# Modulation weights in four buffers of their own, loaded one visit ahead, and both scaled sums on VectorE in four pieces

## The chip, the cores and the metric

The kernel runs on one core of a Trainium2 chip. The metric is the device time of one execution in microseconds (us); the lower the better. The engines are written as in the profile: PE is TensorE (PEld its weight loads), DVE VectorE, ACT ScalarE, POOL GpSimd, SP SyncE, which here issues the transfers.

## The reference, cut to what matters

Two layers (`l` is 0 or 1) of a transformer-like block over 256 latent and 256 context tokens, width 1024. Each layer is a feed-forward block, a token mixer and a second feed-forward block. Before and after each of them the tokens are modulated with vectors that come from two conditioning vectors, `c` for the latent tokens and `c_ctx` for the context tokens:

```python
mx = (silu(c) @ w_mod[l] + b_mod[l]).reshape(B, 9, 1, 1024)
mc = (silu(c_ctx) @ w_mod[l] + b_mod[l]).reshape(9, 1024)
hx = hx + 0.5 * mx[:, 2] * swiglu(modulate(hx, norm_g[l, 0], mx[:, 0], mx[:, 1]), w_gu[l, 0], w_down[l, 0])
...
hx = hx + mx[:, 5] * (ox @ w_out[l])
hx = hx + 0.5 * mx[:, 8] * swiglu(modulate(hx, norm_g[l, 2], mx[:, 6], mx[:, 7]), w_gu[l, 1], w_down[l, 1])
```

`w_mod[l]` has 1024 rows and 9 x 1024 columns, 4 MB for each of the nine vectors `m`; it is used for two input vectors only. `swiglu` is `(silu(x @ gate) * (x @ up)) @ down` with an inner width of 2816.

## The kernel before

**Weights.** All weights come from memory in a fixed list of units (`plan`, line 141). A unit of kind `gu` is 128 gate and 128 up columns (1 MB, two transfers), `down` is 256 output columns of a third of the inner width (1 MB or 768 KB), `mod` is 256 columns of one modulation vector for PE (1 MB), and `dvm` is half of such a quarter for the other engines: two row blocks of 128 by 512 columns (512 KB). Which vectors go by `dvm` is the list `ELEM` (line 35): six of layer 0, and of layer 1 the vectors 0, 4, 3, 5 and 7.

**Loading.** `take` (line 269) hands out the next unit. It first calls `load_to(i + 3)`, which puts the transfers of this unit and of the next two into SP's queue, whatever their kind: `raw` has three buffers, `draw` (for `dvm`) three of 512 KB. SP works its queue in order, and a transfer waits there until its buffer is free.

**Splits.** Matmuls run three times on values that are split in a rounded part and a rest (`mm3`, line 309: lines 312 to 314). `split` (line 254) makes both parts of a weight unit, in two halves: ACT copies (line 265), DVE subtracts (line 266). `spl` has two buffers. `take` splits its own unit if that isn't done, and then calls `ahead` (line 284), which splits the next unit that needs it, but looks no further than two units on.

**The feed-forward loop** (`ffn`, line 733). For each of 22 `gu` units: 48 matmuls of 128x512 (or 128x256 in the last block), `silu` on ACT (line 756), the product `hv` on DVE (line 758), a copy on ACT (line 760) and the rest on POOL (line 761). After 8, 16 and 22 of them four `down` units of 48 or 36 matmuls follow, with four additions of 128x256 on DVE (line 822). After every third step of three matmuls `step` (line 326) is called: it runs one entry of the list `dv`, and then one entry of `q` or one tick of the background work `bg`. In the first block of each layer `bg` is `s5_prep` (line 834), the preparation of the state-space mixer, mostly tensor operations on POOL. Between two units `fillers` (line 301) runs the modulation units that stand there in the list: one `mod` or two `dvm`. So 44 places have two `dvm` in a row; such a place is called a visit. 24 of them lie in the first block of layer 0 (after 16 `gu` and 8 `down` units), 4 in the second, 16 in the first block of layer 1. In 8 of the last 16 only one of the two sums is made.

**What a `dvm` unit does** (`dvm_unit`, line 515). For each of its two row blocks, a sum for `c` on DVE (lines 530 and 532: `acc = raw * scalar + acc`), and one for `c_ctx` in two steps, a scaling on ACT in place (line 535) and an addition on POOL (line 537). All of it is written out at once. After four units PE sums over the partitions (`total`, line 547) and later transposes (`finish`), seven and ten steps on.

**Order.** Nothing is reordered: each engine runs its instructions in the order in which the Python code writes them out.

Of the kernel before, what the change touches and what calls it, by code (L numbers as in the profile page):

```python
# [94 lines left out]
class Net:  # L95
    def __init__(self, nc, tc, I, out, es):
        self.nc, self.tc, self.I, self.out, self.es = nc, tc, I, out, es
        pool = lambda n, b=1, **kw: es.enter_context(tc.tile_pool(name=n, bufs=b, **kw))
        sb = lambda n, b=1: es.enter_context(lines(tc, name=n, bufs=b))
        self.const = sb("const")  # L100
        self.rawp = sb("raw", 3)
        self.splp = sb("spl", 2)
        es.enter_context(tc.tile_pool(name="top", bufs=1, side="right")).tile([128, 8], F32, name="top")
        self.pacc = pool("pacc", 4, space=PSUM)
        self.pt = pool("pt", 3, space=PSUM)
        self.pm = pool("pm", 1, space=PSUM)
        self.bank, self.turn = None, 0
        self.dram = pool("dram", 1, space=DRAM)
        c = self.const
        self.k = c.tile([128, K_END], F32, name="k")  # L110
        self.ident = self.k[:, K_ID:K_ID + 128]
        self.ones = self.k[:, K_ONE:K_ONE + 128]
        self.h = c.tile([128, KT, T], F32, name="h")
        self.xn = c.tile([128, 2, KT, T], F32R, name="xn")
        self.cs = c.tile([128, KT, 38], F32, name="cs")
        self.mh = c.tile([128, 8], F32, name="mh")
        self.sel = c.tile([128, 33], F32, name="sel")
        self.mod = [c.tile([128, 9, KT, 2], F32, name=f"mod{l}") for l in range(2)]
        self.A = [c.tile([128, 3, KT, 2], F32, name=f"A{l}") for l in range(2)]
        self.smT = [c.tile([128, 128], F32, name=f"smT{l}") for l in range(2)]  # L120
        self.kg = [c.tile([128, 4], F32, name=f"kg{l}") for l in range(2)]
        self.rho8 = [c.tile([128, 16], F32, name=f"rho8{l}") for l in range(2)]
        self.units = []
        self.dv = []
        self.fp = None
        self.bg = []
        self.q = []
        self.hold = False
        self.seaming = False
# [11 lines left out]
    def plan(self):  # L141
        I = self.I
        U = self.units

        def mod_units(l, m, us=range(4)):
            for u in us:
                if (l, m) in ELEM:
                    for v in (2 * u, 2 * u + 1):
                        n0, k0 = m * 1024 + v // 4 * 512, v % 4 * 2
                        src = I["w_mod"][l].rearrange("(k p) n -> p k n", p=128)[:, k0:k0 + 2, n0:n0 + 512]  # L150
                        U.append(("dvm", (l, m, v), [(slice(0, 1024), 2, src)], False))
                    continue
                src = I["w_mod"][l].rearrange("(k p) n -> p k n", p=128)[:, :, m * 1024 + u * 256:m * 1024 + u * 256 + 256]
                U.append(("mod", (l, m, u), [(slice(0, 2048), 8, src)], False))

# [12 lines left out]

        def ffn(l, f, fill, skip=0, between=None):
            fill = list(fill)  # L170
            for c in range(3):
                for j in range(max(skip, sum(CH[:c])), sum(CH[:c + 1])):
                    gu(l, f, j)
# [49 lines left out]
    def load_to(self, n):  # L223
        while self.loaded < min(n, len(self.units)):
            i = self.loaded
            kind, key, srcs, sp = self.units[i]
            if kind == "dvm" and self.fp is None:
                return
            if i < 10 and kind == "mod":
                raw = self.prop.tile([128, 2048], F32, name="pmod", tag="pmod", bufs=5)  # L230
            elif kind == "dvm":
                raw = self.fp.tile([128, 1024], F32, name="draw", tag="draw", bufs=3)
            else:
                raw = self.rawp.tile([128, 2048], F32, name="raw", tag="raw")
            for sl, k, src in srcs:
# [33 lines left out]
    def take(self, kind, key, ahead=True):  # L269
# [3 lines left out]
        if self.hold:  # L273
            self.load_to(min(i + 8, 11))
        else:
            self.load_to(i + 3)
        self.split(i)
        if ahead and not self.hold:
            self.ahead()
# [46 lines left out]
    def step(self, n=1):  # L326

        for _ in range(n):
            if self.dv:
                g = self.dv.pop(0)  # L330
                if g:
                    g()
            f = self.q.pop(0) if self.q else None
            if f is not None:
                f()
            else:
                self.tick()
# [6 lines left out]

    def dv_flush(self):
        while self.dv:
            g = self.dv.pop(0)
            if g:
                g()

    def drain(self):
        while self.bg:
# [159 lines left out]
            us = [u] if alone else range(4)  # L512
            self.q.append(lambda: self.mod_finish(l, m, us, e))

    def dvm_unit(self, l, m, v):

        nc = self.nc
        half, r = v // 4, v % 4  # L520
        raw = self.take("dvm", (l, m, v)).rearrange("p (k n) -> p k n", k=2)
        ss = (1,) if l and m > 4 else (0, 1)
        if r == 0:
            self.dacc = {s: self.fp.tile([128, 512], F32, name=f"dacc{s}", tag=f"dacc{s}", bufs=2) for s in ss}
        acc = self.dacc
        for i in range(2):
            c0, c1 = (self.cs[:, 2 * r + i, 6 + s:7 + s] for s in range(2))
            first = r == i == 0
            if first:
                nc.vector.tensor_scalar(acc[1], raw[:, i], c1, None, op0=OP.mult)  # L530
            else:
                nc.vector.scalar_tensor_tensor(acc[1], raw[:, i], c1, acc[1], op0=OP.mult, op1=OP.add)  # L532
            if 0 in ss:
                x = acc[0] if first else raw[:, i]
                nc.scalar.activation(x, raw[:, i], AF.Copy, scale=c0)  # L535
                if not first:
                    nc.gpsimd.tensor_tensor(acc[0], acc[0], x, op=OP.add)  # L537
        if r < 3:
            return
        st = {}  # L540

# [17 lines left out]
            nc.vector.tensor_tensor(dst.rearrange("p (j a) s -> p a j s", a=2), t, bc(b, [128, 2, 2, 2]), op=OP.add)  # L559
            self.mod_derived(l, m, k0, k0 + 4)  # L560

        self.dv_flush()
        self.dv += [None] * 7 + [total, None, None, finish]

    def mod_derived(self, l, m, k0, k1):
        nc = self.nc
# [166 lines left out]
    def ffn(self, l, f, halves, started, nxt=None):  # L733
# [3 lines left out]
        gate = 2 if f == 0 else 8  # L737
        hid = {}
        with lines(self.tc, name=f"ffn{l}{f}", bufs=1) as fp:
            self.fp = fp  # L740
            j0 = 0
            for ci, nf in enumerate(CH):
                for j in range(j0, j0 + nf):
# [10 lines left out]
                                    self.step()  # L754
                    sl = fp.tile([128, T], F32, name="sl", tag="sl", bufs=1)
                    nc.scalar.activation(sl[:, c], pg[:, c], AF.Silu)
                    hv = fp.tile([128, T], F32, name="hv", tag="hv", bufs=2)
                    nc.vector.tensor_tensor(hv[:, c], sl[:, c], pu[:, c], op=OP.mult)  # L758
                    hd = fp.tile([128, 2, T], F32R, name="hid", tag="hid", bufs=8)
                    nc.scalar.activation(hd[:, 0, c], hv[:, c], AF.Copy)  # L760
# [7 lines left out]
                    self.sq_begin()  # L768
                early = None
                if lastc:  # L770
                    self.dv_flush()
                for u in range(4):
                    w = early or self.take("down", (l, f, ci, u))
                    w = w[:, :, 0:nf * 256].rearrange("p s (k n) -> p s k n", k=nf)
# [22 lines left out]
                            self.step()  # L797
                    if ci == 0 and u == 0:
                        self.flush()
                    for i in range(2):  # L800
                        n = 2 * u + i
                        for s in halves:
# [31 lines left out]
    def s5_prep(self, l):  # L834
# [6 lines left out]
        with lines(self.tc, name=f"prep{l}", bufs=1, side="right") as pp:  # L841
# [4 lines left out]
            dma(par[0:16], I["s5_lam_re"][l].rearrange("d (a b) p -> (d a) (b p)", b=2))  # L846
            dma(par[32:48], I["s5_lam_im"][l].rearrange("d (a b) p -> (d a) (b p)", b=2))
            dma(ldt[64:80], I["s5_log_dt"][l].rearrange("d (a b) -> (d a) b", b=2))
            bl = [pp.tile([128, 16, 16], F32, name=f"bl{i}") for i in range(2)]
            for i, nm in enumerate(("s5_b_re", "s5_b_im")):  # L850
                nc.sync.dma_start(bl[i], I[nm][l].rearrange("d (a b) p m -> (b p) (d a) m", b=2))
            cr = pp.tile([128, 4, 2, 2, 64], F32, name="cr", tag="W")
# [824 lines left out]
```

## Time and profile before

| | |
|---|---|
| median of 3 runs | 2185.57 us (2183.81 to 2187.68) |
| profiled execution | 2195.32 us, of which the span of the trace is 2193.5 us |
| mean granted clock of PE | 0.938 |
| PE busy | 1984.7 us, 90% of the span |
| DVE busy | 1109.0 us, 51% |
| ACT busy | 784.7 us, 36% |
| POOL busy | 767.9 us, 35% |
| read from memory | 263.39 MB, 126 GB/s over the span |

The shares are averages over a program with very different stages. What a stage is limited by is read from the idle time of PE inside it, from what ended that idle time, and from the clock that PE was granted there. The modulation visits lie in three stretches of the trace: about 60 to 490 us, 905 to 980 us and 1305 to 1600 us.

### The profile page before, as it was taken

How to read it: one execution, taken by the hardware profiler on the slowest of the kernel's cores; microseconds unless marked ns; L12 is line 12 of the kernel's file. 1: busy time of each engine (PE TensorE's matmuls, PEld its weight loads, DVE VectorE, ACT ScalarE, POOL GpSimd, SP SyncE). 2: the span in 40 equal slices, each digit the busy share in tenths (PEclk: the TensorE clock that was granted, in tenths of full speed). 3: DMA queues.
4: the chain of work that ended last, by engine and by line, in shares of the span. 5: the costliest groups of instructions: out<-in, count | busy, mean ns of one | idle time of the engine just before them, and what ended most of it. 6: DMA issues, size and time to landing. Idle time of an engine off the chain costs nothing. (4 is left out here: it accounts for less than half of the span.)

```text
span 2193.5 us, 27710 instructions
## 1 busy us (share of the span) xinstructions
PE 1984.7 (90%) x10839; PEld 1600.1 (73%) x10839; DVE 1109.0 (51%) x1777; ACT 784.7 (36%) x1283; POOL 767.9 (35%) x789
## 2 busy tenths in 40 slices
PE   7788778889999999989999997778899999899999
PEld 5656556667889568768888875555678888668999
DVE  6566433543655774343332455555543465575554
ACT  4432333332435553331222343321222343455443
POOL 2348766431444404140100224864520244503000
PEclk9888888899999999989999998888899999899999
DMA  7533444454443103443333354344463344308663
GB/s 257 139 116 130 140 135 146 131 162 134 121 157 101 39 4 112 124 143 98 96 96 87 106 140 116 115 134 144 148 188 87 101 132 144 88 20 235 188 190 118
DMA packets 342278, 277.73 MB, mean 127 GB/s; under 512 B 30558, under 2 KB 311460, under 8 KB 342148
## 3 DMA queue, kind: packets, MB, share of 16 engines
q1 hardware_dynamic: 339184, 268.44, 41.2%
q0 software_dynamic: 1888, 7.31, 0.9%
q8 instruction: 85, 1.39, 0.3%
q14 instruction: 45, 0.37, 0.1%
q10 hardware_dynamic: 1076, 0.22, 0.1%
HBM read 263.39 MB, written 12.55 MB: 126 GB/s over the span
## 5 line engine op out<-in xcount | busy, mean ns | idle before, releaser
L312 PE MATMUL acc<-xn,spl 128*128 128x512 f32 (+1 forms) x1664 | 625.3, 376 | 96.3 <-ACT spl L265 87.9
L314 PE MATMUL acc<-xn,spl 128*128 128x512 f32 (+1 forms) x1664 | 617.2, 371 | 20.7 <-DVE spl L266 20.7
L313 PE MATMUL acc<-xn,spl 128*128 128x512 f32 (+1 forms) x1664 | 611.6, 368 | 1.9 <-DVE xn L429 0.2
L266 DVE TENSOR_TENSOR spl<-raw,spl 128x1024 fp32r<-128x1024 f32 (+2 forms) x312 | 391.9, 1292 | 231.5 <-ACT spl L265 229.6
L312 PEld LDWEIGHTS acc<-xn,spl 128*128 128x128 f32 x1664 | 329.0, 198 | 164.9 <-ACT spl L265 98.7
L265 ACT ACTIVATE spl<-raw 128x1024 fp32r<-128x1024 f32 (+3 forms) x344 | 323.8, 989 | 260.3 <-PE acc L314 138.5
L314 PEld LDWEIGHTS acc<-xn,spl 128*128 128x128 f32 x1664 | 327.4, 197 | 89.0 <-DVE spl L266 40.0
L761 POOL TENSOR_TENSOR hid<-hv,hid 128x512 fp32r<-128x512 f32 (+1 forms) x88 | 102.1, 1160 | 783.9 <-ACT hid L760 783.8
L313 PEld LDWEIGHTS acc<-xn,spl 128*128 128x128 f32 x1664 | 329.1, 198 | 54.6 <-DVE xn L658 4.3
L312 PE MATMUL acc<-hid,spl 128*128 128x512 f32 (+1 forms) x740 | 273.3, 369 | 28.8 <-ACT spl L265 28.8
L314 PE MATMUL acc<-hid,spl 128*128 128x512 f32 (+1 forms) x740 | 270.0, 365 | 10.5 <-DVE spl L266 10.5
L313 PE MATMUL acc<-hid,spl 128*128 128x512 f32 (+1 forms) x740 | 268.8, 363 | 0.0
L758 DVE TENSOR_TENSOR hv<-sl,acc 128x512 f32<-128x512 f32 (+1 forms) x88 | 54.6, 621 | 391.5 <-PE acc L314 344.6
L537 POOL TENSOR_TENSOR dacc<-dacc,draw 128x512 f32<-128x512 f32 x126 | 187.2, 1485 | 158.7 <-ACT draw L535 106.8
L822 DVE SCALAR_TENSOR_TENSOR h<-acc,mod,h 128x256 f32<-128x256 f32 x192 | 84.8, 478 | 226.4 <-PE acc L314 226.4
L760 ACT ACTIVATE hid<-hv 128x512 fp32r<-128x512 f32 (+1 forms) x88 | 50.8, 577 | 391.1 <-DVE hv L758 391.1
L312 PEld LDWEIGHTS acc<-hid,spl 128*128 128x128 f32 x740 | 144.0, 195 | 55.4 <-ACT spl L265 32.5
L314 PEld LDWEIGHTS acc<-hid,spl 128*128 128x128 f32 x740 | 144.3, 195 | 37.4 <-DVE spl L266 16.5
L532 DVE SCALAR_TENSOR_TENSOR dacc<-draw,cs,dacc 128x512 f32<-128x512 f32 x154 | 164.0, 1065 | 4.7
L313 PEld LDWEIGHTS acc<-hid,spl 128*128 128x128 f32 x740 | 144.5, 195 | 20.0
L266 POOL TENSOR_TENSOR spl<-raw,spl 128x768 fp32r<-128x768 f32 (+3 forms) x32 | 65.5, 2047 | 213.7 <-ACT spl L265 204.0
L535 ACT ACTIVATE draw<-draw,cs 128x512 f32<-128x512 f32 x126 | 91.0, 724 | 131.4 <-DVE dacc L532 83.2
(390 smaller groups left out, 2355.5 us busy)
## 6 DMA issues: line engine op xcount, KB each, us to landing
raw<-in_ffn_w_gu SPq DMA_DIRECT2D x176, 512.0 KB
draw<-in_w_mod SPq DMA_DIRECT2D x88, 512.0 KB
raw<-in_ffn_w_down SPq DMA_DIRECT2D x32, 1024.0 KB
raw<-in_w_mod SPq DMA_DIRECT2D x20, 1024.0 KB
raw<-in_ffn_w_down SPq DMA_DIRECT2D x16, 768.0 KB
raw<-in_w_in SPq DMA_DIRECT2D x16, 768.0 KB
pmod<-in_w_mod SPq DMA_DIRECT2D x8, 1024.0 KB
raw<-in_w_out SPq DMA_DIRECT2D x8, 1024.0 KB
```

What stands on the lines that cost most here:

```text
L265: nc.scalar.activation(s[:, 0, a:b], raw[:, a:b], AF.Copy)
L266: (nc.gpsimd if mix and b == n else nc.vector).tensor_tensor(s[:, 1, a:b], raw[:, a:b], s[:, 0, a:b].bitcast(F32), op=OP.subtract)
L312: mm(out, sl[0], sr[0], start=start, stop=False)
L313: mm(out, sl[0], sr[1], start=False, stop=False)
L314: mm(out, sl[1], sr[0], start=False, stop=stop)
L532: nc.vector.scalar_tensor_tensor(acc[1], raw[:, i], c1, acc[1], op0=OP.mult, op1=OP.add)
L535: nc.scalar.activation(x, raw[:, i], AF.Copy, scale=c0)
L537: nc.gpsimd.tensor_tensor(acc[0], acc[0], x, op=OP.add)
L758: nc.vector.tensor_tensor(hv[:, c], sl[:, c], pu[:, c], op=OP.mult)
L760: nc.scalar.activation(hd[:, 0, c], hv[:, c], AF.Copy)
L761: nc.gpsimd.tensor_tensor(hd[:, 1, c], hv[:, c], hd[:, 0, c].bitcast(F32), op=OP.subtract)
L822: self.nc.vector.scalar_tensor_tensor(self.h[:, n, c], ps[:, c], self.mod[l][:, gate, n, s:s + 1], self.h[:, n, c], op0=OP.mult, op1=OP.add)
```

## The change

A visit becomes one `dvm` unit of four row blocks instead of two units of two. These units have no transfers in the list any more. `load_to` passes over them, and `take` counts only other units, so that the present and the next two of the others are always asked for. Their transfers (two of 512 KB for a visit) are written out by `dvm_load` one visit ahead, into four buffers of 512 KB, from a list of the visits of this block; the first is written out where the block begins.

`dvm_unit` no longer splits ahead (`take(..., False)`). It finishes the pieces of the visit before, asks for the next visit's load, and puts four pieces into `dv`: each piece is one row block for both vectors, all on DVE. ACT and POOL have no part in it. `total` and `finish` go to a second list `late`, with counts of seven and ten steps, and are forced where their result is needed. `hv` has one buffer instead of two, and the two `bl` tiles of `s5_prep` use a buffer of another tile. Cut to its core:

```diff
@@ plan / mod_units
-                    for v in (2 * u, 2 * u + 1):
-                        n0, k0 = m * 1024 + v // 4 * 512, v % 4 * 2
-                        src = I["w_mod"][l].rearrange("(k p) n -> p k n", p=128)[:, k0:k0 + 2, n0:n0 + 512]
-                        U.append(("dvm", (l, m, v), [(slice(0, 1024), 2, src)], False))
+                    U.append(("dvm", (l, m, u), [], False))
+                    self.visits.setdefault(where[0], []).append((l, m, u))
@@ load_to
-            if kind == "dvm" and self.fp is None:
-                return
+            if kind == "dvm":
+                self.raws[i] = None
+                self.loaded += 1
+                continue
...
-            elif kind == "dvm":
-                raw = self.fp.tile([128, 1024], F32, name="draw", tag="draw", bufs=3)
@@ take
-            self.load_to(i + 3)
+            n, left = i, 3
+            while left and n < len(self.units):
+                left -= self.units[n][0] != "dvm"
+                n += 1
+            self.load_to(n)
@@ step
-                g = self.dv.pop(0)
-                if g:
-                    g()
+                self.dv.pop(0)()
+            for g in self.late:
+                g[0] -= 1
+            while self.late and self.late[0][0] <= 0:
+                self.late.pop(0)[1]()
@@ dvm_load, dvm_unit
+    def dvm_load(self):
+        if not self.todo:
+            return
+        l, m, u = self.todo.pop(0)
+        half, k0 = u // 2, u % 2 * 4
+        self.draws = []
+        for i in range(2):
+            raw = self.fp.tile([128, 2, 512], F32, name="draw", tag="draw", bufs=4)
+            n0 = m * 1024 + half * 512
+            self.nc.sync.dma_start(raw, self.I["w_mod"][l].rearrange("(k p) n -> p k n", p=128)[:, k0 + 2 * i:k0 + 2 * i + 2, n0:n0 + 512])
+            self.draws += [raw[:, 0], raw[:, 1]]
...
-        half, r = v // 4, v % 4
-        raw = self.take("dvm", (l, m, v)).rearrange("p (k n) -> p k n", k=2)
+        half, r = u // 2, u % 2
+        self.take("dvm", (l, m, u), False)
+        raws = self.draws
...
+        self.dv_flush()
+        self.dvm_load()
+        while r == 0 and len(self.late) > 2:
+            self.late.pop(0)[1]()
...
-        for i in range(2):
-            c0, c1 = (self.cs[:, 2 * r + i, 6 + s:7 + s] for s in range(2))
-            first = r == i == 0
-            if first:
-                nc.vector.tensor_scalar(acc[1], raw[:, i], c1, None, op0=OP.mult)
-            else:
-                nc.vector.scalar_tensor_tensor(acc[1], raw[:, i], c1, acc[1], op0=OP.mult, op1=OP.add)
-            if 0 in ss:
-                x = acc[0] if first else raw[:, i]
-                nc.scalar.activation(x, raw[:, i], AF.Copy, scale=c0)
-                if not first:
-                    nc.gpsimd.tensor_tensor(acc[0], acc[0], x, op=OP.add)
-        if r < 3:
+        def parts(i):
+            for s in ss:
+                x = self.cs[:, 4 * r + i, 6 + s:7 + s]
+                if r == i == 0:
+                    nc.vector.tensor_scalar(acc[s], raws[i], x, None, op0=OP.mult)
+                else:
+                    nc.vector.scalar_tensor_tensor(acc[s], raws[i], x, acc[s], op0=OP.mult, op1=OP.add)
+
+        self.dv += [(lambda i=i: parts(i)) for i in range(4)]
+        if r == 0:
             return
...
-        self.dv_flush()
-        self.dv += [None] * 7 + [total, None, None, finish]
+        self.late.append([7, total, m])
+        self.late.append([10, finish, m])
@@ ffn
-            self.fp = fp
+            self.fp, self.todo = fp, self.visits.get((l, f), [])
+            self.dvm_load()
...
-                    hv = fp.tile([128, T], F32, name="hv", tag="hv", bufs=2)
+                    hv = fp.tile([128, T], F32, name="hv", tag="hv", bufs=1)
...
                 if lastc:
-                    self.dv_flush()
+                    self.late_flush()
...
                     if ci == 0 and u == 0:
                         self.flush()
+                        while any(g[2] == 2 for g in self.late):
+                            self.late.pop(0)[1]()
@@ s5_prep
-            bl = [pp.tile([128, 16, 16], F32, name=f"bl{i}") for i in range(2)]
+            bl = pp.tile([128, 2, 16, 16], F32, name="bl", tag="big", bufs=2)
+            bl = [bl[:, i] for i in range(2)]
```

## Rows read from the trace of the kernel before

**Rows 1.** The page, part 1: busy us (share of the span) xinstructions.

```profile
PE 1984.7 (90%) x10839; PEld 1600.1 (73%) x10839; DVE 1109.0 (51%) x1777; ACT 784.7 (36%) x1283; POOL 767.9 (35%) x789
```

**Rows 2.** PE's waits in the whole trace: who, for whom, total, times, longest.

```profile
PE acc L312 <- ACT spl L265: 116.7, 40, 5.5
PE acc L314 <- DVE spl L266: 31.2, 41, 1.6
PE t L1064 <- POOL CL L1057: 8.8, 2, 5.0
```

**Rows 3.** Busy time by stretch; the first line names the columns.

```profile
core 0: us, PE busy (x) PEld busy (x) DVE busy (x) ACT busy (x) POOL busy (x), PEclk, DMA share, GB/s
60.00:490.00 430.00, 344.10 (x1393) 257.32 (x1392) 216.25 (x331) 151.19 (x207) 244.31 (x241) 0.87 0.46 139
165.00:235.00 70.00, 55.65 (x227) 41.48 (x225) 42.23 (x64) 20.15 (x26) 58.54 (x83) 0.87 0.44 144
...
905.00:980.00 75.00, 63.74 (x233) 48.02 (x232) 28.87 (x33) 26.65 (x38) 25.92 (x19) 0.84 0.40 120
1305.00:1600.00 295.00, 235.36 (x975) 175.03 (x973) 167.57 (x246) 79.18 (x110) 169.78 (x177) 0.87 0.43 133
```

**Rows 4.** DVE in order of time, 880 to 920: start, us, what, [idle before <-releaser].

```profile
891.58 0.69 DVE L758 TENSOR_TENSOR hv<-sl,acc 128x512 f32<-128x512 f32 x1 [4.43 <-PE acc L314]
894.18 2.36 DVE L266 TENSOR_TENSOR spl<-raw,spl 128x1024 fp32r<-128x1024 f32 x2 [1.91 <-ACT spl L265]
903.83 0.69 DVE L758 TENSOR_TENSOR hv<-sl,acc 128x512 f32<-128x512 f32 x1 [7.29 <-PE acc L314]
...
916.26 0.69 DVE L758 TENSOR_TENSOR hv<-sl,acc 128x512 f32<-128x512 f32 x1 [8.39 <-PE acc L314]
918.59 2.58 DVE L266 TENSOR_TENSOR spl<-raw,spl 128x1024 fp32r<-128x1024 f32 x2 [1.64 <-ACT spl L265]
```

**Rows 5.** PE in order of time: the first matmul of the 4th and 19th gu unit.

```profile
72.64 0.80 PE L312 MATMUL acc<-xn,spl 128*128 128x512 f32 x1 [3.31 <-ACT spl L265]
...
479.91 0.50 PE L312 MATMUL acc<-xn,spl 128*128 128x512 f32 x1 [2.27 <-ACT spl L265]
```

**Rows 6.** PE in order of time, 325 to 333: after a gap, then ten matmuls on.

```profile
325.31 0.80 PE L312 MATMUL acc<-xn,spl 128*128 128x512 f32 x1 [4.90 <-ACT spl L265]
...
329.85 0.63 PE L313 MATMUL acc<-xn,spl 128*128 128x512 f32 x1
330.28 0.63 PE L314 MATMUL acc<-xn,spl 128*128 128x512 f32 x1
...
332.10 0.39 PE L314 MATMUL acc<-xn,spl 128*128 128x512 f32 x1
332.33 0.39 PE L312 MATMUL acc<-xn,spl 128*128 128x512 f32 x1
```

**Rows 7.** SP's queue, then ACT, in order of time before that gap.

```profile
315.82 2.15 SPq L242 DMA_DIRECT2D raw<-in_ffn_w_gu  x2
...
324.20 2.01 ACT L265 ACTIVATE spl<-raw 128x1024 fp32r<-128x1024 f32 x2 [2.30 <-DMA raw<-in_ffn_w_gu]
```

**Rows 8.** The tile dacc: duration ns min/median/max, first and last start, forms.

```profile
L532 DVE SCALAR_TENSOR_TENSOR dacc<-draw,cs,dacc x154: 736/752/3533, 75.4 to 1600.6; 128x512 f32<-128x512 f32 x154
...
L537 POOL TENSOR_TENSOR dacc<-dacc,draw x126: 1262/1300/2167, 77.0 to 1457.5; 128x512 f32<-128x512 f32 x126
```

**Rows 9.** Groups by line: xcount | busy us, mean ns | idle before, releasers.

```profile
L266 DVE TENSOR_TENSOR spl<-raw,spl 128x1024 fp32r<-128x1024 f32 (+2 forms) x312 | 391.9, 1292 | 231.5 <-ACT spl L265 229.6 <-issue 1.8
...
L822 DVE SCALAR_TENSOR_TENSOR h<-acc,mod,h 128x256 f32<-128x256 f32 x192 | 84.8, 478 | 226.4 <-PE acc L314 226.4
```

**Rows 10.** Busy time by stretch, of line 537 alone: POOL busy, PEclk, DMA share, GB/s.

```profile
60.00:490.00 430.00, 123.88 (x84) 0.87 0.46 139
165.00:235.00 70.00, 19.89 (x14) 0.87 0.44 144
```

**Rows 11.** DVE, then POOL, in order of time, 1503 to 1507.

```profile
1502.94 3.46 DVE L266 TENSOR_TENSOR spl<-raw,spl 128x1024 fp32r<-128x1024 f32 x2 [1.64 <-ACT spl L265]
...
1503.27 2.05 POOL L1076 TENSOR_TENSOR te<-B,pw 128x512 f32<-128x512 f32 x1
```

**Rows 12.** Busy time by stretch, of line 532 alone: DVE busy, PEclk, DMA share, GB/s.

```profile
1305.00:1600.00 295.00, 70.03 (x55) 0.87 0.43 133
```

More of the change, by code (lines that the diff above doesn't have):

```diff
@@ L123, in __init__ @@
         self.units = []
-        self.dv = []
+        self.dv, self.late = [], []
         self.fp = None
@@ L143, in plan @@
         U = self.units
+        self.visits, where = {}, [None]
         def mod_units(l, m, us=range(4)):
@@ L170, in ffn @@
             fill = list(fill)
+            where[0] = (l, f)
             for c in range(3):
@@ L346, in dv_flush, with late_flush @@
         while self.dv:
-            g = self.dv.pop(0)
-            if g:
-                g()
+            self.dv.pop(0)()
+    def late_flush(self):
+        self.dv_flush()
+        while self.late:
+            self.late.pop(0)[1]()
     def drain(self):
@@ L513, in mod_unit, with dvm_unit @@
             self.q.append(lambda: self.mod_finish(l, m, us, e))
-    def dvm_unit(self, l, m, v):
+    def dvm_load(self):
[9 more added lines that the diff above has]
+            self.draws += [raw[:, 0], raw[:, 1]]
+    def dvm_unit(self, l, m, u):
         nc = self.nc
-        half, r = v // 4, v % 4
-        raw = self.take("dvm", (l, m, v)).rearrange("p (k n) -> p k n", k=2)
+        half, r = u // 2, u % 2
+        self.take("dvm", (l, m, u), False)
+        raws = self.draws
         ss = (1,) if l and m > 4 else (0, 1)
+        self.dv_flush()
+        self.dvm_load()
+        while r == 0 and len(self.late) > 2:
+            self.late.pop(0)[1]()
         if r == 0:
@@ L799, in ffn @@
                         self.flush()
+                        while any(g[2] == 2 for g in self.late):
+                            self.late.pop(0)[1]()
                     for i in range(2):
```

## The prediction

> **What bounds the kernel now.** I read four views in turn. The page says that PE is busy 90% of the span [rows 1]: PE sets the time, and only its idle time and its clock can be won. The view of PE's waits says for whom it waits: 40 waits of together 116.7 us for ACT's half of a weight split, and 41 waits of 31.2 us for DVE's half that follows; of the rest only 8.8 us, for the background work on POOL, lies near them [rows 2]. The view by stretches says where: in the three stretches with modulation visits, PE is busy 344.1 of 430 us (A, 60 to 490), 63.7 of 75 (B, 905 to 980) and 235.4 of 295 (C, 1305 to 1600), at a granted clock of 0.87, 0.84 and 0.87 [rows 3]. That is 85.9 + 11.3 + 59.6 = 157 us of idle time.
>
> Why a visit stalls PE is seen where a block goes over from `mod` units to visits. Behind the `hv` of 891.58, with one `mod` unit between two `gu`, DVE runs the next split at 894.18, early in PE's work, and the next `hv` comes 12.4 us before the one at 916.26. At the first visit the split comes only at 918.59, behind that `hv`, which itself waited for the last matmul of its unit [rows 4]. The code says the same: `ahead` looks two units on, and with two `dvm` in a row the next `gu` is the third; it is split in the first `dvm`'s `take`, which is written out behind `hv`. So PE waits for `silu`, `hv`, the copy and half a split each time. Twenty-three units lie between 72.64 and 479.91 [rows 5], 17.7 us each.
>
> Two things add to it. After a gap PE runs at the lower of its two levels for some microseconds: matmuls follow each other every 0.43 us at 330, and every 0.23 us at 332 [rows 6]. And some weights come late, since the two `dvm` count in the three units asked for ahead: in the gap of 4.90 us ACT's split waited for a `gu` transfer that was issued at 315.82 and had landed by 324.20, 8.4 us [rows 6, 7].
>
> **The change part by part, summed against the profiled execution (2195.3 us, span 2193.5).**
>
> *The split moves ahead.* A visit is now one unit, so the next `gu` or `down` is the second in the list, and `ahead` splits it when the unit before is taken, ahead of that unit's matmuls, as at 894.18. The `spl` buffer that it needs is free by then (the unit two back is done). All 44 visits are of this form. What it can give: the idle time, 157 us, and the low clock. The clock of 0.87 in A means that 0.26 of 430 us, 112 us, ran at the low level; likewise 24 us in B and 77 us in C. Of each I take nine tenths as working time (the rest falls into the gaps), in which 0.43 us does the work of 0.23: 0.47 is lost, so 47 + 10 + 32 = 89 us. From the 246 us I leave in the two waits for POOL, 8.8 us, and the slow clock behind them, about 3. The ceiling is 234 us. By it a unit in A takes 17.7 x (430 - 133) / 430 = 12.2 us, and the `mod` units' 12.4 us [rows 4] agree.
>
> *The loads.* As many transfers of the same size are issued. The three `raw` buffers now always hold the present and the next two real units, so a late `gu` (8.4 us from issue to use) has two units, 24 us, of cover. A visit's load stands in SP's queue until DVE has finished the visit before the last; behind it in the queue stands the `raw` load for the third unit on. The visit's load has about a unit, 12 us, against 8.4 us. I cost both at nothing; without the cover a visit would pay what the gap of 4.90 us shows beyond one of 2.27 [rows 5, 6], 2.6 us.
>
> *The sums move to DVE.* 126 additions of 1.3 us (median) leave POOL and 144 scalings leave ACT; neither was on PE's path except through buffers, so this gives nothing by itself. DVE gets 126 more sums of 0.752 us (median) [rows 8] and 18 first products: 95 us and some, 3 us for each of the 36 visits with both vectors. A unit with such a visit then needs on DVE 8 x 0.752 = 6.0 us for sums, 2 x 1.29 for the split and either 0.69 for `hv` or 4 x 0.478 for the additions behind a `down` [rows 4, 8, 9]: 9.3 or 10.5 us, under PE's 12.2. Undisturbed, it hides beside the matmuls. If that cover were gone it would cost up to 3 us for each of 36, 108 us.
>
> *Collisions of DVE and POOL* are what may use it up. The trace has no unit with eight sums, so I bound it. Without the additions of line 537, POOL keeps 244.3 - 123.9 = 120.4 us in A, 38.6 of them in the four units of 165 to 235, and 81.8 in the other twenty [rows 3, 10]: 9.7 and 4.0 us a unit. Lower bound: zero, since DVE has 2 us to spare and the collisions with line 537 vanish (less than zero is covered by the ceiling). Upper bound: every microsecond of POOL holds DVE up. Then the heavy units take 10.5 + 9.7 = 20.2, 8.0 above 12.2, for four units in A and three in C, where the same stage runs for layer 1, and the others of A 10.5 + 4.0 - 12.2 = 2.3, times twenty: 56 + 46 = 102 us. The last eight visits of C have one vector only, 7.5 + 4.0 us, and stay below 12.2. I take a third, 36 us, nearer to zero: where both were at it, two splits took 3.46 us instead of 2.6 and a POOL operation 2.05, against 1.3 for one of its size alone [rows 8, 9, 11], so part of each overlaps. Where PE then waits, the low clock follows; by the ratio above, 89 to 157, this makes 36 into 57 us (bounds 0 and 160).
>
> A rule that bears on this: the Trainium skill, page "SBUF — State Buffer", section "SBUF: two separate sides", calls the port pair of VectorE and GpSimd an exclusive lock, which one holds for its whole instruction while the other fully blocks. The rows just named agree in kind, not in full: 3.46 us is less than 2.6 plus the two POOL operations beside it. By the rule alone the sum would take the first rival's price for the third that I take.
>
> *The rest, with one answer each.* The pieces go out one a step, ahead of the next `hv`; they end three steps before `total`, which then waits for DVE instead of POOL. PE's matmuls are queued behind `total`; this is inside the collision bounds. One `hv` buffer: the next `hv` comes a unit later, the copy and POOL's rest need about 2 us. `bl` shares a buffer whose next user waits for its readers on POOL, the same engine. `late` keeps the steps 7 and 10. All at nothing.
>
> *Sum.* 234 - 57 = 177 us. 2195.3 - 177 = 2018 in a profiled execution, which stood 9.75 us above the median of the runs: 2008 us.
>
> **The rivals.**
>
> 1. *DVE and POOL become the bound wherever POOL prepares the mixer.* If they only take turns, sums and splits (8.6 us) and POOL's share add up: 18.3 us in the seven heavy units, 12.6 in the twenty, 51 us above PE; if everything of DVE is held up, 102. With the clock that is 80 to 160 us, so 2032 to 2112, in the middle 2072. For it: the sums of line 532 average 1.27 us in C [rows 12] against 0.752. Against it: line 537, half of POOL's time in A, is gone, so both engines together do less than before.
> 2. *The change doesn't do what it says:* the splits stay behind `hv`, and only the late loads are mended. The 44 gaps go from a mean of 2.9 to about 2.3 us [rows 2, 5], 26 us and 15 of clock: 2145. Against it stands the code.
> 3. *Slower: the sums outrun the unit.* DVE takes PE's place when eight sums, the split and the additions exceed what a unit takes now: (17.7 - 2.6 - 1.9) / 8 = 1.65 us a sum. At a mean of 2.1 us, a unit takes 21.3, 3.6 above the old one; over 36 visits 130 us, less some 32 that the eight one-vector visits still win: 2284. For it: the longest sum took 3.5 us [rows 8]. Against it: to reach 1.65, POOL must be in the way of almost each sum of every visit, and 4.0 us of POOL a unit can't be.
>
> **How the numbers follow.** Forecast (1948 to 2045): 0.67. Rival 1 (2032 to 2112): 0.22. Rival 2: 0.05. Rival 3: 0.04, and 0.02 that gains and losses cancel. The low end of the range is the ceiling, 2185.6 - 234 = 1952, and a little for gaps that I counted too short; the high end takes in more than half of rival 1 and leaves out the rest: 1948 to 2085. A difference of 0.2% (4 us) is about what a measurement of this kernel can tell from none. Faster 0.94, same 0.02, slower 0.04.
>
> **What would show it.** In the profile after: PE's waits for the ACT half of the split fall from 40 to a few; the clock in the three stretches goes to 0.95 or more; `hv` in B comes every 12 us; the split of a unit runs beside the matmuls of the one before. Line 537's additions and line 535's scalings are gone, and the sums on DVE number 280. If the time is above 2060, PE's waits for DVE's half of the split or for `total` should be found between 165 and 440, with sums of more than 1.2 us. The prediction is wrong in its mechanism if the waits for ACT's half remain, or if new waits for `draw` or `raw` transfers appear.

## The result, and the profile after

| | before | after |
|---|---|---|
| median of the runs | 2186.62 us (4 runs) | 1994.18 us (4 runs, 1993.25 to 1994.99) |
| profiled execution | 2195.32 us | 1994.99 us |
| span of the trace | 2193.5 us | 1993.2 us |
| mean granted clock | 0.938 | 0.976 |

The ratio is 0.912, with a 95% interval of 0.9104 to 0.9135: 8.8% faster. The profiled executions lie 200.3 us apart; the prediction's sum was 177, its range 1948 to 2085. By the medians 192.4 us were won: the profiled execution before stood 8.7 us above its median, the one after 0.8.

The line numbers of the changed kernel differ: the matmuls are lines 316 to 318, the sums 558 and 560, `total` 572, `hv` 784, the matmuls with POOL's background product CL 1093. Part 1 of its page, then PE's waits in the whole trace (the lines that answer to [rows 1] and [rows 2]):

```profile
PE 1892.3 (95%) x10839; PEld 1550.0 (78%) x10839; DVE 1190.9 (60%) x1921; ACT 681.8 (34%) x1139; POOL 625.9 (31%) x663
```

```profile
PE t L1093 <- POOL CL L1086: 29.6, 5, 9.1
PE t L509 <- DMA pmod<-in_w_mod: 7.0, 4, 4.1
PE t L572 <- DVE dacc L560: 6.6, 5, 2.2
...
PE b L572 <- DVE dacc L560: 4.7, 3, 2.7
PE acc L317 <- POOL hid L787: 3.4, 2, 2.4
...
PE acc L318 <- DVE spl L266: 0.5, 1, 0.5
```

The 116.7 us for ACT's half of a split have no line any more, and of the 31.2 us for DVE's half half a microsecond is left. What is on top now is new in size: 29.6 us for CL, against 8.8 before, and 11.3 us in which `total` waits for the sums on DVE.

The same three stretches, each cut where the same work ends (by PE's first matmul behind each block, the blocks that hold A, B and C end 100.9, 123.4 and 200.4 us earlier than before, so the starts and ends are moved by these; PE's counts of matmuls, 1393, 235 and 960 against 1393, 233 and 975, show that the work is nearly the same), and the four heavy units of A; columns as in [rows 3]:

```profile
60.00:389.00 329.00, 298.68 (x1393) 233.55 (x1393) 275.71 (x423) 82.51 (x112) 150.06 (x157) 0.96 0.62 183
805.00:857.00 52.00, 52.00 (x235) 42.04 (x235) 32.78 (x45) 15.94 (x22) 6.52 (x5) 1.00 0.55 164
1182.00:1400.00 218.00, 200.46 (x960) 156.96 (x957) 180.93 (x277) 56.44 (x78) 138.59 (x145) 0.96 0.59 178
165.00:235.00 70.00, 54.58 (x253) 42.27 (x252) 60.59 (x72) 11.66 (x16) 55.47 (x57) 0.88 0.56 165
```

A takes 329 us instead of 430, B 52 instead of 75, C 218 instead of 295: 201 us, all of the gain. It has two parts: PE's idle time fell from 157 to 48 us, and PE's busy time for nearly the same matmuls fell by 45.4, 11.7 and 34.9 us, 92 in all. In B PE has no gap and the full clock. In the last line PE is idle for 15 of 70 us, with DVE at 87% and POOL at 79%: here the two are what PE waits for.

DVE in order of time in B, which answers to [rows 4]; columns as there:

```profile
816.36 0.69 DVE L784 TENSOR_TENSOR hv<-sl,acc 128x512 f32<-128x512 f32 x1 [6.92 <-PE acc L318]
818.70 2.62 DVE L266 TENSOR_TENSOR spl<-raw,spl 128x1024 fp32r<-128x1024 f32 x2 [1.65 <-ACT spl L265]
821.24 0.87 DVE L558 TENSOR_SCALAR dacc<-draw,cs 128x512 f32<-128x512 f32 x2
822.03 4.05 DVE L560 SCALAR_TENSOR_TENSOR dacc<-draw,cs,dacc 128x512 f32<-128x512 f32 x6
827.35 0.69 DVE L784 TENSOR_TENSOR hv<-sl,acc 128x512 f32<-128x512 f32 x1 [1.27 <-PE acc L318]
829.68 2.62 DVE L266 TENSOR_TENSOR spl<-raw,spl 128x1024 fp32r<-128x1024 f32 x2 [1.65 <-ACT spl L265]
832.22 5.38 DVE L560 SCALAR_TENSOR_TENSOR dacc<-draw,cs,dacc 128x512 f32<-128x512 f32 x8
838.34 0.69 DVE L784 TENSOR_TENSOR hv<-sl,acc 128x512 f32<-128x512 f32 x1 [0.73 <-PE acc L318]
```

`hv` comes every 11.0 us. The split looks as it did, 2.3 us behind an `hv`, but it is now the split for the unit after the next: PE has a whole unit between it and its use. All eight sums fit behind it, with 0.7 us to spare.

### The profile page after: what moved, and what is told of

Same layout as the page of the kernel before. It is cut to its first block, busy times and chain, and to the rows that moved or that the text cites. A ratio compares the mean times of both kernels' runs of the same rounds, so it can differ in the third digit from the quotient of the medians.

```text
span 1993.2 us, 27428 instructions
## 1 busy us (share of the span) xinstructions
PE 1892.3 (95%) x10839; PEld 1550.0 (78%) x10839; DVE 1190.9 (60%) x1921; ACT 681.8 (34%) x1139; POOL 625.9 (31%) x663
## 5 line engine op out<-in xcount | busy, mean ns | idle before, releaser
L316 PE MATMUL acc<-xn,spl 128*128 128x512 f32 (+1 forms) x1664 | 598.9, 360 | 8.4 <-ACT mv L1464 6.0
L317 PE MATMUL acc<-xn,spl 128*128 128x512 f32 (+1 forms) x1664 | 589.9, 354 | 1.9 <-DVE xn L438 0.2
L318 PE MATMUL acc<-xn,spl 128*128 128x512 f32 (+1 forms) x1664 | 589.5, 354 | 0.5 <-DVE spl L266 0.5
L316 PEld LDWEIGHTS acc<-xn,spl 128*128 128x128 f32 x1664 | 314.4, 189 | 64.5 <-issue 10.0
L317 PEld LDWEIGHTS acc<-xn,spl 128*128 128x128 f32 x1664 | 314.7, 189 | 50.0 <-DVE xn L683 4.3
L318 PEld LDWEIGHTS acc<-xn,spl 128*128 128x128 f32 x1664 | 314.2, 189 | 47.7 <-DVE spl L266 1.6
L316 PE MATMUL acc<-hid,spl 128*128 128x512 f32 (+1 forms) x740 | 266.6, 360 | 0.0
L317 PE MATMUL acc<-hid,spl 128*128 128x512 f32 (+1 forms) x740 | 263.3, 356 | 3.4 <-POOL hid L787 3.4
L560 DVE SCALAR_TENSOR_TENSOR dacc<-draw,cs,dacc 128x512 f32<-128x512 f32 x280 | 262.9, 993 | 1.1 <-issue 0.2
L318 PE MATMUL acc<-hid,spl 128*128 128x512 f32 (+1 forms) x740 | 263.2, 356 | 0.1
L316 PEld LDWEIGHTS acc<-hid,spl 128*128 128x128 f32 x740 | 140.7, 190 | 23.9 <-issue 5.1
L317 PEld LDWEIGHTS acc<-hid,spl 128*128 128x128 f32 x740 | 140.9, 190 | 23.3 <-POOL hid L787 4.2
L318 PEld LDWEIGHTS acc<-hid,spl 128*128 128x128 f32 x740 | 140.7, 190 | 20.3 <-DVE spl L266 0.5
L316 PE MATMUL acc<-spl,xn 128*128 128x384 f32 (+1 forms) x322 | 111.3, 346 | 0.0
L317 PE MATMUL acc<-spl,xn 128*128 128x384 f32 (+1 forms) x322 | 107.0, 332 | 0.9 <-DVE spl L266 0.6
(387 smaller groups left out, 2155.0 us busy)
```

The source lines that it names most:

```text
L316: mm(out, sl[0], sr[0], start=start, stop=False)
L317: mm(out, sl[0], sr[1], start=False, stop=False)
L318: mm(out, sl[1], sr[0], start=False, stop=stop)
L560: nc.vector.scalar_tensor_tensor(acc[s], raws[i], x, acc[s], op0=OP.mult, op1=OP.add)
```

## The experiments

Every kernel was timed against the kernel before on its own chip; those medians lie between 2186.6 and 2189.5 us.

| kernel | split ahead | loads | second sum on | median us | ratio to before (95%) |
|---|---|---|---|---|---|
| sums_only | no | list, 3 buffers | DVE | 2181.2 | 0.9962 (0.9941 to 0.9982) |
| buf_only | no | list, 4 buffers | ACT, POOL | 2168.3 | 0.9897 (0.9862 to 0.9932) |
| split_back | no | as changed | DVE | 2155.0 | 0.9844 (0.9817 to 0.9871) |
| hoist_only | yes | list, 3 buffers | ACT, POOL | 2219.8 | 1.0144 (1.0105 to 1.0183) |
| hoist_sums | yes | list, 3 buffers | DVE | 2145.1 | 0.9809 (0.9794 to 0.9823) |
| hoist_4buf | yes | list, 4 buffers | ACT, POOL | 2041.2 | 0.9332 (0.9318 to 0.9346) |
| pool_sums | yes | as changed | ACT, POOL | 2043.5 | 0.9345 (0.9331 to 0.9359) |
| at_once | yes | as changed | DVE, at once | 2001.3 | 0.9140 (0.9109 to 0.9170) |
| changed kernel | yes | as changed | DVE, pieces | 1994.2 | 0.9120 (0.9104 to 0.9135) |
| own_load | yes | at the visit, 2 buffers | DVE, pieces | 1994.0 | 0.9102 (0.9072 to 0.9131) |

### Only the split ahead

```diff
+            n, real = i, 0
+            while n < min(i + 4, len(self.units)):
+                real += self.units[n][0] != "dvm"
+                if real > 3:
+                    break
+                n += 1
+            self.load_to(n)
...
         n = min(j + 2, len(self.units))
+        if [x[0] for x in self.units[j:j + 2]] == ["dvm"] * 2 and j + 2 in self.raws:
+            n = j + 3
```

> The kernel before, with one thing added: where two dvm units stand next in the list, the look ahead reaches three units on instead of two (and four units instead of three are asked for, still no more than three of them in raw), so that the next gu or down is split before the matmuls ahead of it. The sums stay where they were (VectorE, ScalarE, GpSimd, all at once), and the loads too. Theory 1 (the place of the split is the gain): most of the 192 us, 2010 to 2060 us; VectorE waits for GpSimd more than in the changed kernel. Theory 2 (taking the second sum off ScalarE and GpSimd is the gain): less than 60 us, over 2125.

Measured: 2219.8 us, 1.4% slower than before. Theory 1's forecast fails by 160 us. The time lies in theory 2's range, which goes by a small gain and not by a loss; `sums_only` and `pool_sums` below speak against its mechanism. ACT's waits for weights in the trace of this kernel:

```profile
ACT spl L265 <- DMA raw<-in_ffn_w_gu: 213.0, 29, 14.4
...
ACT spl L265 <- DMA raw<-in_ffn_w_down: 126.6, 14, 16.7
```

In the kernel before, the same two lines were 25.8 and 64.2 us. The reason is seen in SP's queue, here at one visit; the first view is SP, the second ACT, both in order of time:

```profile
301.55 8.22 SPq L242 DMA_DIRECT2D draw<-in_w_mod  x2
309.82 1.09 SPq L242 DMA_DIRECT2D raw<-in_ffn_w_gu  x2
```

```profile
316.94 2.00 ACT L265 ACTIVATE spl<-raw 128x1024 fp32r<-128x1024 f32 x2 [6.25 <-DMA raw<-in_ffn_w_gu]
318.85 0.58 ACT L764 ACTIVATE sl<-acc 128x512 f32<-128x512 f32 x1
```

The two `draw` transfers hold the queue for 8.2 us, until a buffer comes free (POOL's additions are what this queue waits for most, 588.3 us in the whole trace), and the `gu` behind them is issued only at 309.82. The split, now written out ahead of the unit's `silu`, stands at the head of ACT's queue and waits for it, and everything that ACT owes PE stands behind: PE waits 48 us for `total`'s copy on ACT alone (27.6 + 20.4), which it hadn't done before. Here a split asked for earlier than its weights could come was worse than a late one.

### Only the sums, and the sums at once

```diff
-                nc.scalar.activation(x, raw[:, i], AF.Copy, scale=c0)
-                if not first:
-                    nc.gpsimd.tensor_tensor(acc[0], acc[0], x, op=OP.add)
+                if first:
+                    nc.vector.tensor_scalar(x, raw[:, i], c0, None, op0=OP.mult)
+                else:
+                    nc.vector.scalar_tensor_tensor(acc[0], raw[:, i], c0, acc[0], op0=OP.mult, op1=OP.add)
```

> The kernel before, with the second vector's sums on VectorE instead of ScalarE and GpSimd, all at once as before; splits and loads stay as they were. Theory 1: within 15 us of the kernel before (2170 to 2200), since PE still waits some 2.3 us or more for the split at each visit and the sums come behind the split. Theory 2: 100 us or more faster, under 2087.

Measured: 2181.2 us, 0.4% faster, as theory 1 has it: with the split behind `hv` the sums' place is worth 8 us.

```diff
-        self.dv += [(lambda i=i: parts(i)) for i in range(4)]
+        for i in range(4):
+            parts(i)
```

> The changed kernel, with the four pieces of a visit written out at once, behind hv and ahead of the next split, instead of one a step. Theory 1: VectorE has some 2 us a unit to spare and a split is needed only a unit later, so the order in its queue matters little: 1990 to 2005 us. Theory 3 (the pieces are needed): eight sums of 0.75 us in a row, longer beside GpSimd, push the split and the additions back: 30 us or more slower, over 2024.

Measured: 2001.3 us; the intervals of its ratio and of the changed kernel's overlap. The medians lie 7 us apart, and the pieces' worth isn't told apart from nothing; theory 3 falls. The waits do change place. Those of `total` for the sums, 11.3 us in the changed kernel, are gone from PE's list, and those for DVE's half of the split are back:

```profile
PE acc L318 <- DVE spl L266: 17.8, 9, 3.8
```

### The split put back

```diff
         n = min(j + 2, len(self.units))
+        if j < n and self.units[j][0] == "dvm":
+            return
...
-        self.take("dvm", (l, m, u), False)
+        self.take("dvm", (l, m, u))
```

> The changed kernel, with the split of the unit behind a visit put back to where it was, at the visit, behind hv of the unit before. Loads and sums stay changed. Theory 1: PE again waits for ScalarE's half of the split at each of 44 visits, about 2.3 us, and runs at the lower clock behind it: 2110 to 2170 us. Theory 2: under 2060.

Measured: 2155.0 us, 161 us above the changed kernel and as theory 1 has it, with most of the old waits (PE's, whole trace; 125.6 us of 147.9 before):

```profile
PE acc L318 <- ACT spl L265: 83.8, 33, 3.9
PE acc L320 <- DVE spl L266: 41.8, 44, 2.7
```

So without the split ahead, loads and sums together are worth 33 us against the kernel before on that chip; with it 226 us against `hoist_only`.

### The split ahead with one more buffer, and with either of the other parts

> The kernel before with the look-ahead of three units as in the run hoist_only, and one draw buffer more (four; hv has one buffer and bl shares one, to make room). Transfers stay in the list's order, the sums where they were. Theory 1b: with four buffers a visit's transfers wait for the visit before the last instead of for the last one, so the weights behind them come in time: 2020 to 2100 us. Rival (it is the order of the queue and GpSimd's late additions, not the number of buffers): 2150 us or more.

Its edit is that of `hoist_only`, the room made at `hv` and `bl` as in the changed kernel, and one figure:

```diff
-                raw = self.fp.tile([128, 1024], F32, name="draw", tag="draw", bufs=3)
+                raw = self.fp.tile([128, 1024], F32, name="draw", tag="draw", bufs=4)
```

Measured: 2041.2 us, as theory 1b has it. One buffer of 512 KB more turns 32 us lost into 146 won. ACT's waits for weights, smaller but not gone, and then PE's for POOL and for the split:

```profile
ACT spl L265 <- DMA raw<-in_ffn_w_gu: 42.8, 14, 9.7
ACT spl L265 <- DMA raw<-in_ffn_w_down: 11.2, 5, 4.3
```

```profile
PE t L1073 <- POOL CL L1066: 40.3, 7, 10.5
PE acc L320 <- ACT spl L265: 11.8, 5, 4.1
```

> The kernel before with the look-ahead of three units as in hoist_only, three draw buffers, and both vectors' sums on VectorE, all at once. Draw buffers come free when VectorE is done, without ScalarE and GpSimd behind it. Theory 1b: the transfers still wait for the last visit's sums, so weights still come late: 2100 to 2200 us. Theory 2b (the late additions on GpSimd alone held the buffers): under 2060 us.

This is `hoist_only` with the edit of `sums_only`. Measured: 2145.1 us: better than `hoist_only` by 75 us, but still with weights that come late: ACT's waits for `gu` are even longer, 348.7 us, likely because ACT has no scalings to do meanwhile. SP's queue waits 554.6 us for buffers that sums still need, instead of 655.9. Theory 1b holds; how much of the 75 us comes from buffers that are free sooner was not taken apart.

> The changed kernel, with the second vector's sums put back to ScalarE (scaling) and GpSimd (addition), still in four pieces. Split and loads stay changed. The look-ahead alone had made the kernel before slower, since the split then waited for weights that stood in the queue behind transfers into busy draw buffers. Theory 1b (split ahead and loads out of that queue order are the gain together; the place of the sums is secondary): 2000 to 2040 us, with longer waits for GpSimd's background work than the changed kernel's 29.6 us. Theory 2b (GpSimd must be freed too): 2070 us or more.

```diff
+                if s == 0:
+                    continue
...
+            if 0 in ss:
+                y = acc[0] if r == i == 0 else raws[i]
+                nc.scalar.activation(y, raws[i], AF.Copy, scale=self.cs[:, 4 * r + i, 6:7])
+                if r or i:
+                    nc.gpsimd.tensor_tensor(acc[0], acc[0], y, op=OP.add)
```

Measured: 2043.5 us, 3 us beyond what theory 1b gave, far from theory 2b. What theory 1b said of the background work was wrong in its sign: PE's waits for CL are not longer but shorter, 22.0 us against 29.6; the new waits are for the additions themselves. The time is nearly that of `hoist_4buf`, which gets its weights by a buffer more and not by loads of their own; that the two ways are worth the same is likely and not shown, since there the sums are written out at once and here in pieces. The sums on DVE win 49 us over this kernel; `hoist_4buf`, whose loads and pieces differ too, lies 47 us above the changed kernel. PE waits here for the additions on POOL:

```profile
PE t L584 <- POOL dacc L572: 28.0, 7, 13.5
PE t L1105 <- POOL CL L1098: 22.0, 7, 7.3
PE b L584 <- POOL dacc L572: 19.7, 2, 14.5
```

In the block with B, where POOL prepares nothing, the changed kernel, `hoist_4buf` and `pool_sums` take the same 377.8 us between the ends of two blocks; what the sums' place is worth lies in the blocks with A and C, beside the background work.

### The buffer alone, and the load at the visit

> The kernel before with one draw buffer more (four; hv has one and bl shares one, to make room) and nothing else: splits, order of transfers and sums as before. If the fourth buffer is worth something only together with the look-ahead (theory 1b): the late weights are mended, no more than the 26 us and 15 us of clock that the prediction's second rival counted, 2145 to 2187 us. Rival (the buffer alone holds the gain of 180 us between hoist_only and hoist_4buf): under 2120 us.

Its edit is the figure and the room of `hoist_4buf`. Measured: 2168.3 us, 1.0% faster, as theory 1b has it. The buffer alone mends the late weights and little else; ACT's waits for `gu` fall from 25.8 to 6.8 us, and those for `down` from 64.2 to 3.7.

> The changed kernel, with each visit's transfers written out at that visit instead of one visit ahead, into two buffers of half a visit instead of four. They then wait for the pieces of the last visit as well. Theory 1b says that what counts is that no gu or down stands behind a busy draw buffer when its split is due: the weights are asked for two units ahead, so they still come in time, and the pieces only start later; 1994 to 2015 us. Rival (the load a visit ahead is needed): VectorE waits for draw transfers at the head of its queue and holds up splits and hv: 2040 us or more.

```diff
-            raw = self.fp.tile([128, 2, 512], F32, name="draw", tag="draw", bufs=4)
+            raw = self.fp.tile([128, 2, 512], F32, name="draw", tag="draw", bufs=2)
...
-        raws = self.draws
         ss = (1,) if l and m > 4 else (0, 1)
         self.dv_flush()
         self.dvm_load()
+        raws = self.draws
...
-            self.dvm_load()
```

Measured: 1994.0 us, the same as the changed kernel. With loads outside the list, neither the four buffers nor the visit ahead is what counts. By the code of both kernels, every `gu` and `down` is asked for two units ahead, in front of the visit's transfers and not behind them.

### What is left: CL, and DVE beside POOL

> The changed kernel, with eleven empty ticks more between the background work's first CL products on GpSimd and TensorE's first matmuls with them. If those waits, 29.6 us in the changed kernel's trace and the lower clock behind them, are just GpSimd being late where its work is densest, and the ticks at the end of the block are free: waits under 12 us, 1965 to 1980 us. Rival (the lateness is carried along or GpSimd's work is needed as late as before elsewhere): 1988 to 1998 us.

```diff
-                pk = self.tp()
...
+                    if hg == 0:
+                        for _ in range(0 if d else 11):
+                            yield
+                        pk = self.tp()
```

Measured: 1986.3 us (0.9067 to 0.9097 of before), between the two forecasts. Of 29.6 us of waits 12.3 are left, just over what was expected, but only 8 us were won of the 14 to 29 expected. (The edit also takes the PSUM tile `pk` only behind the ticks.)

> As late_cl, with two empty ticks more ahead of the matmuls with each of the three later CL products too. In late_cl 12.3 us of waits for CL were left, 4.0 and 3.0 us of them at the later products. If those are short of time by their ticks only: waits under 6 us and 1976 to 1984 us. Rival (the time is given back in other waits between VectorE and GpSimd): 1984 to 1990 us.

```diff
+                    for _ in range((11, 2, 2, 2)[2 * d + hg]):
+                        yield
+                    if hg == 0:
+                        pk = self.tp()
```

Measured: 1975.7 us (0.8992 to 0.9051 of before; the changed kernel's interval begins at 0.9104). The waits for CL no longer occur in PE's list; the time is a little below the forecast. Of the kernels that make both sums this is the fastest.

> The changed kernel, with one sum instead of two at all 44 visits (the sum for the context vector is left out, the other one is used for both), so VectorE has half the sums to do in the stretches with background work. If the waits left there (for CL on GpSimd, for the sums in total) come from VectorE and GpSimd getting in each other's way: 1960 to 1975 us, waits for CL under 20 us. Rival (GpSimd is late because TensorE now comes past its ticks sooner, whatever VectorE does): 1985 to 1994 us, waits for CL about 30 us.

```diff
-        ss = (1,) if l and m > 4 else (0, 1)
+        ss = (1,)
```

This kernel leaves out a sum that the block needs and is a measurement only. Measured: 1968.7 us (two runs), in the first theory's range; PE's wait for CL stays at its size, as the rival has it, and those of `total` are gone from the list:

```profile
PE t L1093 <- POOL CL L1086: 27.6, 4, 10.8
PE t L509 <- DMA pmod<-in_w_mod: 7.3, 4, 4.1
```

So there are two separate remainders. POOL is late for CL also with half of DVE's sums gone; that PE now passes the ticks sooner than POOL can work them off fits this and `late_all`, where ticks alone took the waits away. And that half of DVE's sums costs about 25 us, of which 11.3 are the waits of `total`; how the rest comes about was not taken apart.

## Why the prediction was right, point by point

*What bounds the kernel, and the split ahead.* Right. The waits for both halves of the split are gone, `split_back` brings most of them back with 161 us, and the clock in A, B and C went from 0.87, 0.84, 0.87 to 0.96, 1.00, 0.96.

*The loads "cost nothing".* This step was wrong in what it left out. I asked whether the changed loads would be late, and they aren't. I didn't ask whether the split ahead would work with the old ones. It doesn't: alone it costs 32 us, and loads out of the old order (or one buffer more) are worth 179 us to it (2219.8 against 2041.2). The order in SP's queue that I named as a risk of the change was the fault of the kernel before. The first reading, that late weights were a small addition to the stall, came from a trace in which the late split hid how late they were: ACT's waits for the two weights were 90 us there and 340 in `hoist_only`.

*The sums "give nothing by itself".* Right by itself (0.4%), and incomplete: once the split is out of the way, leaving POOL is worth 49 us, since PE would wait for the additions there next (47.7 us in `pool_sums`).

*The ceiling and the collisions.* From 246 us I took 8.8 us of waits and 36 of collisions, 45 in all, and 24 for the clock behind them. Measured, PE is idle for 30.3 us in A (329 - 298.68) and 17.5 in C (218 - 200.46), 48 in all; 246 - 48 = 198, and 200.3 was won. So the total of the idle time was sized right, and the clock term, 24 us, was the one that was off: the busy time that came back is 92 us, where the low clock of the kernel before had been priced at 89 and 24 of them were to be lost again. That the totals of idle time agree is luck: 8.8 us were taken over for CL, and it is 29.5; 36 were put down for collisions, and the waits of `total` for the sums are 11.3 (the rest of the 48 are 3.4 us for POOL's rest of `hid`, 3.0 for `par`, a small tile of the background work, and 0.5 for the split). Of the 48 us, 27 are two pairs of waits for CL (line 1093: 9.14 and 4.30 us in A, 9.03 and 4.30 in C), and a low clock inside a wait costs nothing. The ratio of slow clock to idle time, 89 to 157, held for 44 short stalls and not for a few long ones.

*Whom the remaining waits are for.* Half right. I expected PE to wait for DVE, held up by POOL. The larger part is PE waiting for POOL itself. The view by stretches of the changed kernel shows both engines near their limit at 165 to 235; the two waits, and POOL's work just ahead of the first:

```profile
195.53 0.64 PE L1093 MATMUL t<-CL,BB 128*32 128x128 f32 x2 [9.14 <-POOL CL L1086]
200.47 1.10 PE L1093 MATMUL t<-CL,BB 128*32 128x128 f32 x14 [4.30 <-POOL CL L1086]
```

```profile
191.37 1.18 POOL L1084 TENSOR_TENSOR te<-CT,pw 128x576 f32<-128x576 f32 x1
192.50 1.16 POOL L1085 TENSOR_TENSOR te<-CT,pw 128x576 f32<-128x576 f32 x1
193.74 1.73 POOL L1086 TENSOR_TENSOR CL<-te,te 128x576 f32<-128x576 f32 x1
```

POOL works almost without a pause there. The collisions are real: the sums on DVE have a mean of 0.993 us in this view of groups by line, against a median of 0.744:

```profile
L560 DVE SCALAR_TENSOR_TENSOR dacc<-draw,cs,dacc 128x512 f32<-128x512 f32 x280 | 262.9, 993 | 1.1 <-issue 0.2
```

POOL is the cause: sorted by what it does meanwhile, the 169 of the 280 sums with no operation of POOL beside them took 0.753 us at most, and the 111 with one took 1.376 us on average. It shows by stretch too, as least, median and longest time in ns, in B, where POOL is busy for 6.5 of 52 us, and in the four heavy units of A, where it is busy for 55.5 of 70:

```profile
L560 DVE SCALAR_TENSOR_TENSOR dacc<-draw,cs,dacc x23: 737/739/742, 822.0 to 856.5; 128x512 f32<-128x512 f32 x23
L560 DVE SCALAR_TENSOR_TENSOR dacc<-draw,cs,dacc x32: 736/886/3639, 164.3 to 231.5; 128x512 f32<-128x512 f32 x32
```

*The rivals.* The first, DVE and POOL as the bound, is what limits the four heavy units and not the stretch. The second's price for the late loads, 41 us, was twice what `buf_only` showed (21). The third needed 1.65 us a sum; 0.99 was measured, and 1.09 in the four heavy units of A.

## What to carry to other kernels

A step that is written out earlier needs its inputs earlier: before moving it, follow the queue that brings them, and see what stands there ahead of them and for whose buffer that waits. Two edits that are each worth little or less than nothing can be worth most of the gain together, so price them in pairs. When the main wait is gone, look at the background work that is spread by the loop's steps: a faster loop passes its points sooner, and some empty ticks where that work is densest were worth another 18 us here.

## What the runs showed of the hardware that was not expected

Behind one long wait the lower clock costs little. At 195 us, 9.1 and 4.3 us of waiting lie in one stretch of low clock; its two ends, in stretches of 2 us with columns as in [rows 3]:

```profile
187.00:189.00 2.00, 0.00 (x0) 0.00 (x0) 2.00 (x3) 0.00 (x0) 1.98 (x2) 0.92 1.19 305
189.00:191.00 2.00, 0.00 (x0) 0.00 (x0) 2.00 (x3) 0.00 (x0) 1.92 (x4) 0.50 0.46 111
...
205.00:207.00 2.00, 2.00 (x9) 1.58 (x8) 1.79 (x3) 1.47 (x2) 2.00 (x2) 0.81 1.10 357
```

That is some 17 us of low clock, and PE is idle for about 11 of them, so the clock of 0.88 at 165 to 235 is mostly idle time; nine matmuls of 128x512 behind the waits, from 201.49 to 205.50, went at 0.43 us each instead of 0.23, some 2 us lost. Behind the many short waits of the kernel before, the low level fell on working time: with the waits gone, nearly the same matmuls took 92 us less in A, B and C.

Sums on DVE of more than 0.76 us occur in the changed kernel's trace only with an operation of POOL beside them: 89 of 111 such sums, the longest of 3.64 us. The other 22 took no longer than the 169 sums that had POOL idle beside them, 0.75 us.
